# Attention scores with stacked keys and both query halves on every row, and weighted values in one slice

## The chip, the cores and the metric

The kernel runs on one core of a Trainium2 chip. The metric is the device time of one execution in microseconds. Five engines share the work: PE multiplies matrices (PEld is its weight load, a queue of its own in the profile), DVE and ACT do elementwise work, POOL does some elementwise work and issues transfers, SP only issues transfers.

## The reference

Two layers of a diffusion backbone over 256 context tokens and 1024 latent tokens, width 1024. Layer 0 is a pair of recurrent mixers and a mixture of experts; layer 1 is windowed attention and a second mixture of experts. Only the attention of layer 1 is touched:

```
for each block of 128 latent queries, 16 query heads in 4 key groups, head size 64:
    s_loc = q . k          over the latent keys within +-128 tokens (up to 384 keys)
    s_ctx = q . k_ctx      over all 256 context keys
    p     = softmax([s_loc, s_ctx, sink of the head])
    o     = p[:, :window] . v  +  p[:, window:-1] . v_ctx
out = o @ w_out
```

All inputs are f32. The kernel makes most f32 products out of short-significand parts: x is split into hi (x rounded) and lo = x - hi, and hi.hi, hi.lo and lo.hi are added in PSUM.

## The kernel before

Layer 1 is projected token tile by token tile; rotated queries and keys go out to DRAM with channels on rows, two key groups (64 channels each) on the 128 rows of a tile. `keys` brings the keys back in two parts: `k2` holds the hi part of a key group twice, on both row halves, and `kl` the lo part, two groups on one tile. `load_q` brings the queries of a query tile and a pair of key groups: for each group, the hi part stands on the group's own row half and the lo part on the other half.

`Attn.run` goes through 64 steps of one query tile, one key group and two heads each (8 steps for a query tile), and 12 more that finish what is in flight. PE's order is that of the code (a manual schedule); on ACT, DVE and POOL the framework's scheduler sets the order. In a step PE does, in turn:

- the scores of a first head (L1902 against the window's keys, L1903 against the context's), in two passes: `k2` on all 128 rows (hi.hi + lo.hi at once), and then `kl` on the group's 64 rows (hi.lo);
- transposes of probabilities of two steps before (L1937, into `ps_pT`);
- the scores of the second head, and the rest of the transposes;
- a slice of the weighted values (`mix`, L1954, into `ps_av`; the stationary operand has 64 columns). A `mix` serves two steps and comes in two slices, two key blocks in the first and the rest in the second, so every step has one;
- a slice of the output projection of an earlier query tile (`out_tile`, L1345, six products), and now and then transposes, router product (L1396) and affinities of a tile.

Around it, DVE masks and reduces the scores (L1910), ACT takes the exponentials (L1915), DVE and ACT make the scale (L1918 to L1922: a sum on ACT's side, a reciprocal on DVE's), ACT scales one head (L1924) and POOL or DVE the other (L1923). ACT copies the transposes' first and last tile out of PSUM (L1941), DVE the middle one (L1939); they take turns in two PSUM buffers. Once in four steps the next queries are split (ACT L1876, DVE L1877). Behind the fifth query tile DVE also begins the list of best tokens of each expert (L1421 to L1430), a slice in each step.

When the last query tile is through its router (L1396, L1400), DVE makes the second list, rows are gathered, and the second mixture of experts starts; its weights have been loaded ahead.

Of the kernel before, what the change touches and what calls it, by code (L numbers as in the profile page):

```python
# [10 lines left out]
F32R = mybir.dt.float32r  # L11
# [8 lines left out]
D = 1024  # L20
# [11 lines left out]
def step_of(m):  # L32
    """Step at which direction 1 meets chunk m, and the chunk of a step."""
    return 3 - m if m < 4 else 23 - m
# [6 lines left out]
def rows_ap(t, off, rows, cols):  # L41
    """rows x cols view of a contiguous DRAM tensor, from element `off`."""
    return bass.AP(tensor=t.tensor, offset=t.offset + off, ap=[[cols, rows], [1, cols]])
# [12 lines left out]
def log_exp_table(K):  # L56
    """Loads the activation table that serves Ln and Exp together."""
    K.table = K.tc.keep_in_program_order(K.nc.scalar.preload_act_table_set("natural_log_exp_and_others")).ins


def behind(K, ins, name):
    """Keeps an instruction behind the named one in program order."""
    K.tc.add_manual_dep(ins.ins, name, mybir.DependencyInfo(
        mybir.DependencyClass.NoSync, mybir.DependencyReason.DATA), reason="order")


def after_table(K, ins):
    """Keeps an activation behind the last explicit table load."""
    if ins.ins.name not in K.pinned:
        K.pinned.add(ins.ins.name)  # L70
        behind(K, ins, K.table.name)


class Fill:
    """Generators advanced beside a main stream, one slice at a time; lead: instructions they are moved forward."""
# [26 lines left out]
# ---------------------------------------------------------------- constants  # L102
# [4 lines left out]
def consts(K, A):  # L107
# [9 lines left out]
    # per 64-row half: free index minus row index of the half  # L117
# [48 lines left out]
    # silu(c), silu(c_ctx) as [128 d, k, 32] stationaries with two live columns  # L166
# [6 lines left out]
# ---------------------------------------------------------------- ada modulation  # L173
def ada_part(K, A, layer, jj, wp, pp, wtag="adaw", ptag="adap", bufs=2):
    """N-chunks 4jj..4jj+3 of layer's modulation rows: rows 32g (lat), 32g+1 (ctx) of modr[:, jj]."""
# [37 lines left out]
def modcol(K, layer, m, kt, s):  # L213
    """[128,1] column of modulation m for channels 128kt.., stream s (0 lat, 1 ctx)."""
# [4 lines left out]
def mod_bcast(K, layer, m, s, dst):  # L219
    """dst [128, D] <- modulation m of stream s on every partition."""  # L220
# [6 lines left out]
def norm_cols(K, pool, layer, norm, ms, mh, tag):  # L227
    """[128, 2, kt, stream]: gain * (1 + scale), shift of a modulated norm; ms, mh: scale and shift modulations."""
# [11 lines left out]
# ---------------------------------------------------------------- layer-0 input: norm, modulate, transpose  # L240
def head(K, A, hp, hh, hl):
    """hh + hl = modulated RMS norm of [ctx; x], channel layout [128, 8, T]."""
# [61 lines left out]
# ---------------------------------------------------------------- layer-0 projection, column tile by column tile  # L304
def both(nc, out, ps, func, **kw):
    """Activation of a projected column tile (context, latent) into token order."""
# [4 lines left out]
class InProj:  # L311
    """Projected column tiles (first column, continuation), weights loaded two tiles ahead across runs."""
# [28 lines left out]
    def run(self, posts, fills, drain):  # L341
        """Continues the next tiles with posts; fills: (generators, slices per k tile); drain: those to finish."""
# [23 lines left out]
def post_z(K, j, wk, tag, bufs):  # L366
    """Stores the silu of gate tile j."""
# [9 lines left out]
# ---------------------------------------------------------------- RWKV-7 operands  # L377
def store_L(K, unit, n0, x, rev=False):
    """x [(half, s), chunk, t] -> K.s_L [unit, chunk, half, s, t]; chunks n0.. (descending if rev)."""
# [3 lines left out]
class Rwkv:  # L383
    """Token shift, loras, decays and the chunk operands alpha, rho, beta, kappa of both directions.

    With c the running sum of the log decay inside a chunk, in the direction's order:
    alpha = kk e^(c-), rho = r e^c, beta = b e^-c, kappa = k e^-c.
    """
# [26 lines left out]
    def shift(self, ps, j, out):  # L415
        """out = (1 - mu) p + mu/2 (previous + next), zero beyond the ends of each stream."""
# [29 lines left out]
    def invert(self, ct):  # L446
        """Queues the inverses of a column tile once its chunk matrices are traced."""
# [5 lines left out]
    def prep_gen(self, ct):  # L453
# [14 lines left out]
        for bi, (a, m) in enumerate(BLK):  # L468
# [75 lines left out]
            # bonus and gate  # L544
# [28 lines left out]
# ---------------------------------------------------------------- gated DeltaNet operands  # L573
class Gdn:
    """Short convolution, gates and the chunk matrices of the gated delta rule, keys and queries not normalised.

    With nk = 1/|k|: L[t,s] = (k_t.k_s) e^(g_t-g_s) nk_s^2 beta_s, A[t,s] = (q_t.k_s) e^(g_t-g_s) nk_s^2 beta_s,
    r = v/nk - e^g S k, Y = (I+L)^-1 r, o = q S e^g + A Y, S' = e^(gl) S + (k nk^2 beta e^(gl-g))^T Y.
    Rows 0-63 carry direction 0, rows 64-127 direction 1 in flipped token order.
    """  # L580
# [12 lines left out]
    def to_chunks(self, ps, src, w):  # L593
        """ps [(d, p), step, w] <- src [128 token, tile, d, w], direction 1 flipped."""
# [20 lines left out]
    def gates(self, ab):  # L615
# [11 lines left out]
        # softplus(x) = max(x, 0) + ln(1 + e^-|x|)  # L627
# [33 lines left out]
    def conv(self, ps, j):  # L661
        """Five-tap centred convolution over tokens of column tile j."""
# [40 lines left out]
    def sums(self, sq, s, h):  # L703
        """K.ssq[tok, tile, s, h] = sum over channels of the squares, plus eps."""
# [23 lines left out]
    def tok(self, x, h, c0, scaled):  # L728
        """Channel tile x -> token rows of K.s_kv [T, 1024], columns of head h (values divided by nk)."""
# [60 lines left out]
# ---------------------------------------------------------------- inverses of the 32-blocks of I + L  # L790
def inv_blocks(K, c0):
    """The tensor of the inverses of chunk c0, its number of chunks and the place of c0 in it."""
# [3 lines left out]
def tri_inv(K, pool, parts, store, bufs=2):  # L796
    """Inverts the two 32-row diagonal blocks of 64x64 chunk matrices, one block per lane.

    parts: (unit, swap, first chunk, chunks), lanes (chunk, half, q) each. K.s_L holds L^T (L where swap is set);
    K.s_T [form, unit, chunk, half, q, 32, 32] receives the inverse (form 0) and its transpose (form 1), chunks  # L800
    of the context and of the latent tokens apart.
    """
# [38 lines left out]
# ---------------------------------------------------------------- the two scans, chunk by chunk  # L841
def scan_rows(K):
    """K.rows: token rows of each step, rows 0-63 forward, rows 64-127 backward; and rows of K.s_o[0 or 1]."""
# [15 lines left out]
class Scan:  # L859
# [14 lines left out]
    def tri_tile(self, n):  # L874
        """Tile of the inverses of step n, its zero blocks set."""
# [9 lines left out]
    # -- loads  # L885
    def load2(self, m):
        """Channel operands of steps 2m, 2m+1."""
# [24 lines left out]
    def load_tri(self, n):  # L912
        """Inverse blocks of step n."""
# [14 lines left out]
    def load_tok(self, n):  # L928
        """Token operands of step n."""
# [14 lines left out]
    # -- matrices that do not wait for the state  # L944
    def gram(self, n):
        """Chunk products of the RWKV operands of step n, and their operands on token rows; six slices."""
# [32 lines left out]
    def corner(self, n):  # L979
        """The off-diagonal 32-block -T22 L21 T11 of every inverse of step n; six slices."""  # L980
# [161 lines left out]
    def run(self, later, tri):  # L1142
        """All steps; later: called with a load of a later step; tri: inverses that only latent steps need."""
# [31 lines left out]
# slices of a step: r and n the two recurrences, g and c the matrices of the next step between them  # L1175
# [5 lines left out]
# ---------------------------------------------------------------- scan outputs -> mixer output, channel layout  # L1181
def split_hl(K, hi, lo, src):
    """hi = src rounded to the short significand, lo = src - hi."""
# [4 lines left out]
def post_rwkv(K, p, ps, mh, ml, ct, a, m, o):  # L1188
    """Generator: loads, mean, variance and the rest."""
# [26 lines left out]
def post_gdn(K, p, ps, mh, ml, tt, o_):  # L1216
    """Generator: the normed rows, then their turn into channel layout."""
# [27 lines left out]
def turns(posts):  # L1245
    """Slices of the generators of a block (one slice in already), a later one between the two of each."""
# [4 lines left out]
def load_split(K, wp, W, rows, cols, name, parts, bufs=3, tag="wstage", gain=None, stage=None, now=True):  # L1251
    """Resident hi/lo [128, rows/128, cols] of a DRAM matrix; parts: (k tile, partition, nrows, row0) pieces.

    gain: factors of the columns, on every partition; with now False the third result is a generator that loads and
    splits, one k tile a slice.
    """
# [26 lines left out]
def tile_rows(t, tt):  # L1283
    """Rows of token tile tt of a (context, latent) pair of DRAM tensors."""
# [3 lines left out]
def load_raw(K, t, W, last):  # L1288
    """t [128, 8, 1024] <- a square matrix, to be split later; issued behind instruction last."""
# [12 lines left out]
def bcast_mods(K, A, layer, s, cpool, tpool, ps, ms, norm, tag, tb=2, shared=None):  # L1302
    """Modulations ms of stream s on every partition; the first one as norm gain * (1 + scale) if norm is given."""
# [20 lines left out]
def out_tile(K, p, op, ps2, ps1, m, wh, wl, tt, x_src, g2, nrm, router, aff, bufs=2, tb=2, t0=0, halves=False):  # L1324
    """Out projection of token tile tt, residual, FFN norm, router affinities of the tile; a generator.

    Slices: eight of the product, then two turns, the router product and the affinities.

    m(k): hi and lo of channel tile k of the branch; halves: the product is made one half of the columns after the
    other, in one bank.  # L1330
    g2: gate of the branch on every partition, or None where the weights carry it. K.s_h holds the normed rows
    before the modulation nrm.
    """
# [384 lines left out]
class Attn:  # L1718
# [226 lines left out]
    def mix(self, n, pair, jj, pTs):  # L1945
# [5 lines left out]
        for c, ch in enumerate(chunks):  # L1951
# [4 lines left out]
            if c in (1, len(chunks) - 1):  # L1956
                yield
# [381 lines left out]
```

## Time and profile before

| | |
|---|---|
| median of 3 runs | 3622.27 us (3619.68 to 3623.23) |
| span of the profiled execution | 3620.5 us |
| what lies around it, median less span | 1.8 us |
| mean granted TensorE clock | 0.943 |
| busy: PE, DVE, ACT, POOL | 92%, 67%, 57%, 20% |
| attention steps, first scores to the end of the last ones | 2563 to 2942 us |

The time of the profiled execution is not listed apart from its span; 1.8 us is taken for what lies around it. PE's busy share counts pipelined matmuls with modelled ends, so what a matmul costs PE is read from the distance between starts, not from its duration. PEclk 1.00 is 2.4 GHz, 0.50 is 1.2 GHz.

### The profile page before, as it was taken

What the parts mean: (1) busy time and instruction counts of PE and PEld (TensorE: products, weight loads), DVE (VectorE), ACT (ScalarE), POOL (GpSimd) and SP (SyncE); (2) the same over time, 40 slices, a digit from 0 to 9 for tenths busy, and PEclk for the clock granted to TensorE, in tenths of its full rate; (3) what the DMA queues carried; (4) which work ended last, traced back from release to release, by engine and by line L of the source; (5) the groups of instructions that cost most, each with busy time, mean ns of one, the idle gap of its engine ahead of it and who ended that gap; (6) DMA issues with size and microseconds to landing.
All of it is one profiled execution on the core that took longest, in us unless ns stands there. A gap on an engine that the chain in (4) does not pass through costs nothing. (4 is left out here: it accounts for less than half of the span.)

```text
span 3620.5 us, 60293 instructions
## 1 busy us (share of the span) xinstructions
PE 3343.5 (92%) x23392; PEld 2475.0 (68%) x23392; DVE 2421.4 (67%) x4034; ACT 2073.4 (57%) x3529; POOL 731.6 (20%) x716
## 2 busy tenths in 40 slices
PE   5999999996999979699999999899899986999997
PEld 3866667775888867566666666567667764888885
DVE  4267774667343356967777777644666588999998
ACT  4244554332333356376666666453577745888886
POOL 1233322222322244111111100101223310101001
PEclk8999999996999989899999999999699997999998
DMA  5255565666897756468888887663311138999995
GB/s 190 70 190 172 183 204 172 225 187 126 172 210 162 162 167 209 152 245 282 282 288 278 284 286 265 202 230 123 77 39 44 47 110 306 378 396 386 394 375 217
DMA packets 480161, 767.80 MB, mean 212 GB/s; under 512 B 231836, under 2 KB 318532, under 8 KB 472708
## 3 DMA queue, kind: packets, MB, share of 16 engines
q1 hardware_dynamic: 434640, 601.05, 50.2%
q0 software_dynamic: 41648, 151.55, 13.5%
q10 hardware_dynamic: 3587, 11.36, 1.0%
q8 instruction: 184, 3.01, 0.3%
q14 instruction: 102, 0.83, 0.1%
HBM read 631.48 MB, written 132.38 MB: 211 GB/s over the span
## 5 line engine op out<-in xcount | busy, mean ns | idle before, releaser
L1185 DVE TENSOR_TENSOR ulo<-raw,uhi 128x1024 fp32r<-128x1024 f32 x768 | 901.6, 1222 | 127.6 <-ACT uhi L1184 118.9
L1184 ACT ACTIVATE uhi<-raw 128x1024 fp32r<-128x1024 f32 x768 | 789.4, 1069 | 245.2 <-PE ps_y L1624 127.0
L1573 PE MATMUL ps_h<-uhi,xh 128*128 128x512 f32 x1024 | 333.7, 404 | 1.4 <-ACT uhi L1184 1.3
L1573 PE MATMUL ps_h<-ulo,xh 128*128 128x512 f32 x1024 | 320.4, 393 | 3.0 <-DVE ulo L1185 1.0
L1573 PE MATMUL ps_h<-uhi,xl 128*128 128x512 f32 x1024 | 319.0, 392 | 0.0
L1640 POOL DMA_INDIRECT s_x<-yo,idxl x31 | 49.2, 1587 | 977.1 <-DVE yo L1636 977.1
L1573 PEld LDWEIGHTS ps_h<-uhi,xh 128*128 128x128 f32 x1024 | 184.0, 188 | 73.5 <-ACT uhi L1184 21.4
L1573 PEld LDWEIGHTS ps_h<-ulo,xh 128*128 128x128 f32 x1024 | 190.6, 188 | 54.9 <-DVE ulo L1185 12.4
L1573 PEld LDWEIGHTS ps_h<-uhi,xl 128*128 128x128 f32 x1024 | 191.2, 188 | 41.5
L354 PE MATMUL ps_in<-hl,whi 128*128 128x512 f32 x512 | 172.2, 411 | 0.0
L354 PE MATMUL ps_in<-hh,wlo 128*128 128x512 f32 x512 | 169.4, 409 | 1.5 <-POOL wlo L338 1.5
L354 PE MATMUL ps_in<-hh,whi 128*128 128x512 f32 x512 | 169.5, 408 | 0.9 <-DVE convu L671 0.9
L1624 PE MATMUL ps_y<-uhi,th 128*128 128x512 f32 x512 | 167.2, 407 | 0.6 <-ACT tc L1610 0.5
L1624 PE MATMUL ps_y<-ulo,th 128*128 128x512 f32 x512 | 161.1, 395 | 0.1
L1624 PE MATMUL ps_y<-uhi,tl 128*128 128x512 f32 x512 | 158.7, 391 | 0.0
L1910 DVE CUSTOM_DVE_ANT_0 pe<-ps_s,amask,sink 128x640 f32<-128x640 f32 (+2 forms) x128 | 104.4, 816 | 66.7 <-PE ps_s L1903 65.0
L966 DVE TENSOR_TENSOR ar<-ps_g,strict 64x256 f32<-64x256 f32 x80 | 33.8, 422 | 154.2 <-PE ps_g L964 153.9
L1923 POOL TENSOR_SCALAR pe<-pe,ast 128x640 f32<-128x640 f32 (+1 forms) x48 | 92.1, 1919 | 215.1 <-DVE ast L1922 193.7
L1546 ACT ACTIVATE xv<-ps_x,Gf 128x128 f32<-128x128 f32 x256 | 96.7, 471 | 66.7 <-PE ps_x L1542 66.7
L1579 PE MATMUL ps_hc<-raw,xc 128*32 128x512 f32 x1024 | 126.1, 599 | 0.0
L1624 PEld LDWEIGHTS ps_y<-uhi,th 128*128 128x128 f32 x512 | 91.1, 188 | 49.7 <-issue 20.1
L1345 PE MATMUL ps_out<-woh,mh 128*128 128x512 f32 x288 | 117.6, 454 | 0.0
(509 smaller groups left out, 7548.9 us busy)
## 6 DMA issues: line engine op xcount, KB each, us to landing
raw<-in_moe_w_dram SPq DMA_DIRECT2D x384, 1024.0 KB
ada_w<-in_ada_w_dram SPq DMA_DIRECT2D x48, 1024.0 KB
wraw<-in_e_w_in_dram SPq DMA_DIRECT2D x32, 512.0 KB
s_rk<-arbk POOLq DMA_DIRECT2D x16, 1024.0 KB, 5.7
kq<-s_kq SPq DMA_DIRECT2D x20, 512.0 KB
s_x<-ox POOLq DMA_DIRECT2D x18, 512.0 KB
s_h<-ot POOLq DMA_DIRECT2D x18, 512.0 KB, 4.1
s_rkv<-rkv POOLq DMA_DIRECT2D x12, 640.0 KB, 3.9
```

The costliest lines, as they stand in the source:

```text
L354: nc.tensor.matmul(ps, l[:, k, :], r[:, k, a:a + m], start=(k == 0 and n == 0), stop=(k == 7 and n == 2))
L966: nc.vector.tensor_mul(ar[orow, hp, :, cd[d]], pg[orow, :, 0:64], K.strict[orow, d:d + 1, :].to_broadcast([64, 4, 64]))
L1184: K.nc.scalar.activation(hi, src, AF.Copy)
L1185: K.nc.vector.tensor_sub(lo, src, hi)
L1345: nc.tensor.matmul(po[:, cp_], l, r[:, k, c_], start=(k == 0 and n == 0), stop=(k == 7 and n == 2))
L1546: nc.scalar.activation(v[:, q], pt[:, q], AF.Identity, bias=self.nrm[:, 1, k, 0:1], scale=self.nrm[:, 0, k, 0:1])
L1573: nc.tensor.matmul(pl[m][n], l[:, k], r[:, 512 * n:512 * n + 512], start=(k == 0 and i == 0), stop=(k == 7 and i == 2))
L1579: nc.tensor.matmul(pc[32 * g:32 * g + 32], xc[:, k_], rs[g // 2][:, 512 * (g % 2):512 * (g % 2) + 512], start=(k_ == 0), stop=(k_ == 7), s ...
L1624: nc.tensor.matmul(py[n], l[:, k], r[:, 512 * n:512 * n + 512], start=(k == 0 and i == 0), stop=(k == 7 and i == 2))
L1640: nc.gpsimd.indirect_dma_start(out=K.s_x[1], out_offset=bass.IndirectOffsetOnAxis(ap=idx[:, e:e + 1], axis=0), in_=yo, in_offset=None, com ...
L1910: nc.vector.tensor_tensor_reduce(pe[:, a:b], sc[:, 512 - nl + a:512 - nl + b], self.mask[:, m:m + b - a], 1.0, low, OP.add, OP.min, st[:, ...
L1923: (nc.vector if n < NV else nc.gpsimd).tensor_scalar(pes[0][:, :nk], pes[0][:, :nk], st[:, 4, 0:1], None, op0=OP.mult)
```

## The change

The keys of a group stand as hi on the group's own row half and lo on the other half, in one tile; `kl` is gone. The queries of a group stand as hi on both halves and, in a second tile, as lo on both halves. The scores are two passes over all 128 rows: queries hi against keys (hi.hi + hi.lo), then queries lo against the same keys (lo.hi, and lo.lo, which was left out before). Each load of queries has two ACT copies and two DVE subtractions for a group instead of one each; each part of the keys has one ACT copy less for a group. `mix` makes all its products in one slice, so of two steps one has them all and the other none, and what follows a `mix` comes one step earlier.

```diff
@@ keys
-            self.kl = p.tile([128, 2, T], F32R, name="kl", bufs=1)
...
-                r = slice(64 * par, 64 * par + 64)
-                for half in range(2):
-                    nc.scalar.activation(self.k2[64 * half:64 * half + 64, 2 * a + par, c], t[r], AF.Copy)
-                nc.vector.tensor_sub(self.kl[r, a, c], t[r], self.k2[r, 2 * a + par, c])
+                r, o = slice(64 * par, 64 * par + 64), slice(64 * (1 - par), 64 * (1 - par) + 64)
+                nc.scalar.activation(self.k2[r, 2 * a + par, c], t[r], AF.Copy)
+                nc.vector.tensor_sub(self.k2[o, 2 * a + par, c], t[r], self.k2[r, 2 * a + par, c])
@@ load_q
-        q2 = p.tile([128, 2, 4, 128], F32R, name="q2", tag="q2", bufs=2)
+        q2 = p.tile([128, 2, 2, 4, 128], F32R, name="q2", tag="q2", bufs=2)
...
-            nc.scalar.activation(q2[r, g], t[r], AF.Copy)
-            nc.vector.tensor_sub(q2[o, g], t[r], q2[r, g])
+            for x in (r, o):
+                nc.scalar.activation(q2[x, 0, g], t[r], AF.Copy)
+            for x in (r, o):
+                nc.vector.tensor_sub(q2[x, 1, g], t[r], q2[r, 0, g])
@@ probs
-            qa = q2[:, gg, 2 * jj + i_]
-            for i, (l, r) in enumerate(((qa, self.k2[:, g]), (qa[hr], self.kl[hr, pair]))):
-                nc.tensor.matmul(sc[:, 512 - nl:512], l, r[:, k0:k0 + nl], start=(i == 0), stop=(i == 1))
-                nc.tensor.matmul(sc[:, 512:768], l, r[:, 0:NCTX], start=(i == 0), stop=(i == 1))
+            k2 = self.k2[:, g]
+            for i in range(2):
+                qa = q2[:, i, gg, 2 * jj + i_]
+                nc.tensor.matmul(sc[:, 512 - nl:512], qa, k2[:, k0:k0 + nl], start=(i == 0), stop=(i == 1))
+                nc.tensor.matmul(sc[:, 512:768], qa, k2[:, 0:NCTX], start=(i == 0), stop=(i == 1))
@@ mix
-            if c in (1, len(chunks) - 1):
-                yield
+        yield
@@ run, mix_step
-            mx, left, key, jj_ = mixes[0]
-            if left == 2 and jj_ == 0:
+            mx, key, jj_ = mixes.pop(0)
+            if jj_ == 0:
                 self.av = pso.tile([128, 4, 128], F32, name="ps_av", tag="av")
-            next(mx, None)
-            mixes[0][1] -= 1
-            if left == 1:
-                mixes.pop(0)
-                if jj_ == 1:
+            next(mx)
+            if jj_ == 1:
...
```

PE in the middle of the attention, the scores of a first head between an output-projection slice and the transposes. Before:

```order
L1345 MATMUL ps_out<-woh,ml 128x512
L1902 MATMUL ps_s<-k_22547,q_24430 128x384
L1903 MATMUL ps_s<-k_22547,q_24430 128x256
L1902 MATMUL ps_s<-kl,q_24430 128x384
L1903 MATMUL ps_s<-kl,q_24430 128x256
L1937 MATMUL ps_pT<-ident,pe 128x128 x4
```

Now (the lines have moved by one; `k_22547` now holds hi and lo):

```order
L1345 MATMUL ps_out<-woh,ml 128x512
L1903 MATMUL ps_s<-k_22547,q_24477 128x384
L1904 MATMUL ps_s<-k_22547,q_24477 128x256
L1903 MATMUL ps_s<-k_22547,q_24477 128x384
L1904 MATMUL ps_s<-k_22547,q_24477 128x256
L1938 MATMUL ps_pT<-ident,pe 128x128 x4
```

The number of products and their columns are as before; the second pass no longer takes another tile on half of the rows. Behind the second head's scores the two steps of a `mix` read on PE, before:

```order
L1937 MATMUL ps_pT<-ident,pe 128x128 x6
L1954 MATMUL ps_av<-pT,v 64x256 x4
L1345 MATMUL ps_out<-woh,mh 128x512
...
L1937 MATMUL ps_pT<-ident,pe 128x128 x6
L1954 MATMUL ps_av<-pT,v 64x256 x6
L1345 MATMUL ps_out<-woh,mh 128x512
```

and now:

```order
L1938 MATMUL ps_pT<-ident,pe 128x128 x6
L1955 MATMUL ps_av<-pT,v 64x256 x10
L1345 MATMUL ps_out<-woh,mh 128x512
...
L1938 MATMUL ps_pT<-ident,pe 128x128 x6
L1345 MATMUL ps_out<-woh,mh 128x512
```

The ten products stand in one step, and in the other the projection follows the transposes at once. (A product shown here is two records in the profile.) On ACT, the queries of a load in the middle of the attention, before:

```order
L1924 ACTIVATE pe<-pe,ast 128x640
L1320 ACTIVATE rst<-rst 128x1
L1876 ACTIVATE q_24430<-qld 64x512 x2
L1941 ACTIVATE pT<-ps_pT 128x512
L1915 ACTIVATE pe,ast<-pe,ast 128x640
```

and now, a step and a half of it:

```order
L1942 ACTIVATE pT<-ps_pT 128x512
L1916 ACTIVATE pe,ast<-pe,ast 128x640
L1875 ACTIVATE q_24477<-qld 64x512
L1942 ACTIVATE pT<-ps_pT 128x256
L1916 ACTIVATE pe,ast<-pe,ast 128x640
L1920 ACTIVATE ast<-ast 128x2
L1875 ACTIVATE q_24477<-qld 64x512
L1391 ACTIVATE ohT<-ps_hT,Gf_22896 128x128 x4
L1925 ACTIVATE pe<-pe,ast 128x640
```

Of the four copies of a load, one now stands between the two exponentials of a step and ahead of a copy of transposes, others stand between the sum (L1920, before L1919) and the scaling (L1925, before L1924).

## Rows read from the trace of the kernel before

**Rows 1.** Busy time by engine in three stretches of the attention: stretch, length, busy (instructions).

```profile
core 0: us, PE busy (x) PEld busy (x) DVE busy (x) ACT busy (x) POOL busy (x), PEclk, DMA share, GB/s
2563.20:2633.60 70.40, 65.30 (x250) 43.05 (x251) 57.77 (x117) 44.55 (x95) 21.33 (x10) 0.59 0.29 76
2633.60:2900.50 266.90, 266.90 (x1623) 187.50 (x1622) 163.84 (x432) 196.44 (x461) 83.71 (x50) 1.00 0.12 41
2900.50:2942.30 41.80, 41.78 (x260) 30.33 (x258) 35.87 (x123) 26.24 (x69) 12.10 (x10) 1.00 0.11 39
```

**Rows 2.** The same stretches, line L1902 alone: four products are one step.

```profile
2563.20:2633.60 70.40, 27.55 (x48) 13.59 (x49) 0.59 0.29 76
2633.60:2900.50 266.90, 72.78 (x176) 32.77 (x177) 1.00 0.12 41
2900.50:2942.30 41.80, 11.44 (x32) 5.76 (x31) 1.00 0.11 39
```

**Rows 3.** PE and PEld in order of time, one step: start, duration, instruction, [idle before].

```profile
2748.02 0.19 PEld L1902 LDWEIGHTS ps_s<-k,q 128*128 128x128 f32 x1
2748.02 0.39 PE L1345 MATMUL ps_out<-woh,ml 128*128 128x512 f32 x1
2748.24 0.34 PE L1902 MATMUL ps_s<-k,q 128*128 128x384 f32 x1
2748.41 0.28 PE L1903 MATMUL ps_s<-k,q 128*128 128x256 f32 x1
2748.62 0.18 PEld L1902 LDWEIGHTS ps_s<-kl,q 64*128 64x128 f32 x1 [0.19 <-issue]
2748.62 0.44 PE L1902 MATMUL ps_s<-kl,q 64*128 64x384 f32 x1
2748.90 0.27 PE L1903 MATMUL ps_s<-kl,q 64*128 64x256 f32 x1
2749.10 0.66 PE L1937 MATMUL ps_pT<-ident,pe 128*128 128x128 f32 x4
2749.51 0.42 PE L1902 MATMUL ps_s<-k,q 128*128 128x384 f32 x1
2749.77 0.28 PE L1903 MATMUL ps_s<-k,q 128*128 128x256 f32 x1
...
2750.46 0.88 PE L1937 MATMUL ps_pT<-ident,pe 128*128 128x128 f32 x6
```

**Rows 4.** PE in order of time around the two slices of a `mix`.

```profile
2756.45 0.87 PE L1937 MATMUL ps_pT<-ident,pe 128*128 128x128 f32 x6
2757.26 1.08 PE L1954 MATMUL ps_av<-pT,v 128*64 128x256 f32 x8
2758.27 0.50 PE L1345 MATMUL ps_out<-woh,mh 128*128 128x512 f32 x1
2758.61 0.39 PE L1345 MATMUL ps_out<-wol,mh 128*128 128x512 f32 x1
...
2762.80 1.52 PE L1954 MATMUL ps_av<-pT,v 128*64 128x256 f32 x12
```

**Rows 5.** Groups of 2633.6 to 2900.5 on ACT and DVE: busy, mean ns, idle before.

```profile
L1924 ACT ACTIVATE pe<-pe,ast 128x640 f32<-128x640 f32 x46 | 38.1, 829 | 18.9 <-DVE ast L1922 18.9
L1876 ACT ACTIVATE q<-qld 64x512 fp32r<-64x512 f32 x23 | 14.3, 623 | 0.2
...
L1877 DVE TENSOR_TENSOR q<-qld,q 64x512 fp32r<-64x512 f32 x22 | 15.1, 686 | 0.7
```

**Rows 6.** PE in order of time: the first two heads' scores of the attention.

```profile
2563.24 0.58 PE L1902 MATMUL ps_s<-k,q 128*128 128x256 f32 x1 [1.01 <-ACT qst L1831]
...
2564.69 0.58 PE L1902 MATMUL ps_s<-k,q 128*128 128x256 f32 x1
```

**Rows 7.** The key operands by tile: count, duration ns min/median/max, first and last start.

```profile
L1751 ACT ACTIVATE k<-kT x16: 732/735/739, 2492.1 to 2559.5; 64x640 fp32r<-64x640 f32 x16
```

**Rows 8.** DVE in order of time: first token list's start and end, last tile's router.

```profile
2899.64 0.82 DVE L1421 MAX8 tk<-aff 16x8 f32<-16x640 f32 x1
...
2976.34 0.21 DVE L1430 TENSOR_SCALAR tk<-tk 16x128 f32<-16x128 f32 x1
...
2982.82 0.17 DVE L1400 TENSOR_REDUCE sm<-ps_rt 128x1 f32<-128x16 f32 x1 [6.27 <-PE ps_rt L1396]
```

**Rows 9.** Busy time in the stretch of that token list, columns as in rows 1.

```profile
2899.60:2976.50 76.90, 70.94 (x422) 51.40 (x420) 69.64 (x202) 38.70 (x98) 17.23 (x14) 1.00 0.29 101
```

**Rows 10.** The same for one expert of the second mixture of experts.

```profile
3168.50:3203.60 35.10, 34.99 (x160) 28.49 (x160) 32.60 (x33) 29.73 (x39) 3.10 (x2) 1.00 1.03 393
```

More of the change, by code (lines that the diff above doesn't have):

```diff
@@ L1892, in probs @@
         st = p.tile([128, 5, 2], F32, name="ast", tag="ast", bufs=4)
-        hr = slice(64 * gg, 64 * gg + 64)
         h0 = 4 * g + 2 * jj
@@ L1980, in mix_step @@
                 return
-            mx, left, key, jj_ = mixes[0]
-            if left == 2 and jj_ == 0:
+            mx, key, jj_ = mixes.pop(0)
+            if jj_ == 0:
                 self.av = pso.tile([128, 4, 128], F32, name="ps_av", tag="av")
-            next(mx, None)
-            mixes[0][1] -= 1
-            if left == 1:
-                mixes.pop(0)
-                if jj_ == 1:
-                    mh, ml = (p.tile([128, 4, 128], F32R, name=x, tag=x, bufs=3) for x in ("mh", "ml"))
-                    split_hl(self.K, mh, ml, self.av)
-                    m[key] = mh, ml
-                    if key[1] == 1:
-                        outs.append([out(key[0], [m.pop((key[0], x)) for x in range(2)]), 0])
+            next(mx)
+            if jj_ == 1:
+                mh, ml = (p.tile([128, 4, 128], F32R, name=x, tag=x, bufs=3) for x in ("mh", "ml"))
+                split_hl(self.K, mh, ml, self.av)
+                m[key] = mh, ml
+                if key[1] == 1:
+                    outs.append([out(key[0], [m.pop((key[0], x)) for x in range(2)]), 0])
         ng = self.load_q(0, 0)
@@ L2030, in run @@
                 else:
-                    mixes.append([self.mix(ty, pair_, jj_, (first, pT)), 2, (ty, pair_), jj_])
+                    mixes.append([self.mix(ty, pair_, jj_, (first, pT)), (ty, pair_), jj_])
             if i % 4 < 3:
```

## The prediction

> **What bounds the kernel now.** I read the stretches first: the change touches the attention alone, and a busy share of the whole span says nothing about it. The 64 steps fall into three stretches [rows 1, 2]. The first 12 (48 products of L1902, four to a step) take 70.4 us at a granted clock of 0.59, with PE idle for 5.1 us of it and DVE for 12.6. The next 44 take 266.9 us, 6.07 us a step, at the full clock, and PE has no idle time at all, while ACT is idle 70.5 us (1.60 a step) and DVE 103. The last 8 take 41.8 us; PE is full there too, and DVE is busy for 35.9.
>
> So PE sets the time of the 44 steps. What it does in one I read from the order of time, by distances between starts, since the durations overlap [rows 3]. The first head's scores go from 2748.24 to the transposes at 2749.10: 0.86 us. The first two products, on all rows, are 0.17 apart, and the second one, of 256 columns, should then need little more than 0.12 (twelve records of 256 columns and eight differ by four records and 1.52 - 1.08 = 0.44 us, so 0.11 each [rows 4]). It takes 0.21 until the next product starts. The weight load of that next product, the one on 64 rows, was idle for 0.19 us with nothing to wait for, and starts together with its product, whereas the load for the first product starts with the projection's last product, 0.22 us ahead of its own. So when the pass goes from 128 rows to 64, the load does not run beside the product before it; and again on the way back (0.28 and 0.20 for the two products on 64 rows). The second head, behind transposes, takes 0.95 (2749.51 to 2750.46), as its first interval is 0.26.
>
> A `mix` slice shows the same at its ends [rows 4]. Six transposes take 0.81 us before it, where four before a score take 0.41, which is 0.62 for six: 0.19 more. The slice of eight records takes 1.01, eight times 0.11 is 0.88: 0.13 more. The first product of the projection behind it takes 0.34 against 0.22 [rows 3]: 0.12 more. That is 0.44 for a slice.
>
> **The change, part by part.** *Scores on PE.* Without the changes of rows a head costs 0.17 + 0.12 + 0.17 + 0.12 = 0.58 us, and 0.67 behind transposes. Against 0.86 and 0.95 that is 0.28 a head, 0.56 a step. If the first weight load of the transposes then also hides behind the last product (one transpose is 0.41 / 4 = 0.10), it is 0.38 a head, 0.76 a step. *The mix.* One slice of 0.44 in two steps goes, 0.22 a step; where the projection now follows transposes directly, its first product may take the 0.09 by which 0.26 is above 0.17: 0.17 a step. Together PE has 0.73 to 0.98 us less in a step of 6.07.
>
> One rule of the Trainium skill speaks against that. "TensorE: Matmul & The Clock Gate", in the section "The mechanism" under "Packing small matmuls", says that a weight load overlaps a running product only when their row groups differ. By it the change would lose 0.13 us a head (worked out with the rivals) where the rows give a gain of 0.28. The trace disagrees: the load of 2748.02 and its predecessor's product are both on 128 rows and start together [rows 3].
>
> *The queries.* Each load, once in four steps, has two more ACT copies of 0.623 us and two more DVE subtractions of 0.686 [rows 5]: 0.31 and 0.34 us a step. They are hidden by ACT's 1.60 and DVE's 2.3 idle us of a step as long as PE is the longest. But the step shrinks too, so ACT becomes the next bound: 1.60 - 0.31 = 1.29 us of idle time are left, and of that 0.43 a step (18.9 / 44) is ACT waiting for DVE's reciprocal, a round trip that a shorter PE does not remove. So ACT allows 0.86 to 1.29, by how much of the trip the copies now placed there fill. PE allows 0.73 to 0.98. With two engines that close, one step with all of a `mix` and one with none, and only two buffers for the transposes, some of it is lost: in the short step PE runs ahead, and its last transposes stand behind ACT's copy of the first ones, which waits in ACT's queue behind an exponential or a scaling (0.83 us [rows 5]). A copy that comes 0.6 us late in one of two steps costs 0.3 a step. I take **0.70 a step**, near PE's lower bound less a little, with 0.40 and 0.98 as ends: 44 x 0.70 = **31 us** (18 to 43).
>
> *The first 12 steps.* At half clock a head takes 1.45 us [rows 6], four products of 256 columns at twice 0.11 are 0.88, so PE could give 0.57 x 24 = 14 us. But DVE has 12.6 us idle here, and three loads of queries add 3 x 1.37 = 4.1, so it allows at most 8.5, and PE already waits for others in 5.1 us. I take half, **4 us** (0 to 9).
>
> *The last 8 steps and the 12 that finish.* PE's gain is the same 0.73 to 0.98 a step, but DVE is busy with the first token list from 2899.64 to 2976.34 [rows 8], 69.6 of 76.9 us [rows 9], and the last tile's router finds it idle only for 6.27 us. The list starts when a tile's affinities are there and moves forward with them. So up to 7.3 + 6.3 us can be taken out between the two before DVE is the bound, less 1.4 for a load: 12 us, and PE would take out 8 x 0.85 = 7. Placement will cost some: I take **4 us** (0 to 8). In the finishing steps five slices of a `mix` become fewer by two at 0.44: **1 us**.
>
> *The keys.* The second part of the keys stands between the projection and the first scores. Four ACT copies of 0.735 [rows 7] go there, 2.9 us; the first scores wait for ACT [rows 6], but for its query copy, with DVE's rotation between. I take **2 us** (0 to 3). The first part lies beside the projection and costs nothing: PE works on there.
>
> Behind the attention all that follows waits for the last tile's router, and an expert keeps PE busy for 34.99 of 35.10 us [rows 10], from weights loaded ahead, so it moves forward whole and gives nothing back.
>
> Sum: 31 + 4 + 4 + 1 + 2 = 42 us, off the profiled span of 3620.5 and the 1.8 us around it, which is the median of 3622.3: **3580 us**. The ends add up to 18 + 0 + 0 + 0 + 0 = 18 and 43 + 9 + 8 + 1 + 3 = 64: 3604 and 3558.
>
> **The rivals.** *ACT takes over the bound* (a wait in place of the one removed). For it: 196.4 + 44 x 0.31 = 210 us of ACT work against 266.9 - 31 = 236, 89%, in one fixed order with a copy of queries ahead of a copy of transposes. Against it: its idle time now is mostly waiting for PE. If a step gains 0.15 to 0.40 only, that is 7 to 18 us there and about 4 elsewhere: 3600 to 3612, say 3605.
>
> *DVE gives it back at the end*: if the token list ends later than the last router, the 7 us of the last 8 steps and part of the 31 stay in DVE's queue. That needs the list to be late by more than its 6.27 us of slack; it would cost 5 to 10 us and end at about 3588, inside the main case's range.
>
> *The clock* (the other side). In the first 12 steps the granted clock was 0.59 with PE busy for 65.3 of 70.4 us, so busy does not mean full clock. If PE, now waiting for ACT, were granted 1.2 GHz in the later steps, a step would take twice the distances above: two heads at 2 x 0.58, ten transposes at 0.20, ten records of a `mix` at 0.22, six projection products at 0.44, or 2.3 + 2.0 + 2.2 + 2.6 = 9.1 us, 3.0 above today's and 3.7 above the forecast. Twelve such steps use up the gain of 42; twenty would give 3580 + 74 = 3654. Against it: in an expert DVE and ACT work nearly as long as PE and in turn with it, and the clock is 1.00 [rows 10].
>
> *Loads that do not hide*: if a load on 128 rows could not run beside a product on 128 rows, four loads of 0.10 would stand open in each head, 0.58 + 0.41 = 0.99 us against 0.86, so 128 heads lose 0.13 each and the slices still gain 0.2 x 52: 3622 + 17 - 10 = 3629. The load of 2748.02 speaks against it [rows 3]. This is the rule of "TensorE: Matmul & The Clock Gate" above.
>
> *The change does little*: if the 0.2 us gaps come from the alternation of the two products' banks and not of rows, only the `mix` gains: 3622 - 10 = 3612.
>
> **How the numbers follow.** Main case (with the late list) 0.66, ACT as the bound 0.20, gaps that stay 0.05, the clock 0.04, loads 0.02, more than 64 us 0.03. Leaving out the last four and the upper part of the ACT case, the range is 3557 to 3606. A change below 0.2% (7 us) cannot be told from none with this kernel: slower 0.05, within 0.03, faster 0.92.
>
> **What would show it.** Right: starts of the scores' products 0.17, 0.12, 0.17, 0.12 apart, no idle time of the load ahead of the second pass, steps of about 5.4 us, PE with a few short waits for ACT's copies of transposes, the full clock from the thirteenth step on, and the same 35.1 us an expert. Wrong: distances of 0.2 that stay; long PE waits for ACT; a granted clock under 1.00 between the thirteenth step and the end of the attention; a router wait on DVE behind the first list.

## The result and the profile after

The changed kernel takes 3594.7 us (median of 4 runs, 3592.2 to 3602.1) against 3622.7 (3619.7 to 3623.2): ratio 0.993, 95% interval 0.9914 to 0.9946. The profiled execution took 3594.87 us, its span is 3593.0 (27.5 less than before), the mean granted clock 0.947. The forecast was 3580 us in 3557 to 3606: faster, as said, but the gain is 28 us instead of 42.

Where the 27.5 us of span came from is read from the same stretches as before, from the first scores to step 12, to step 56, and to the last scores. Busy time by engine in them, columns as in [rows 1], after:

```profile
2563.10:2625.70 62.60, 45.58 (x256) 36.26 (x257) 58.16 (x119) 45.40 (x99) 20.41 (x10) 0.78 0.34 89
2625.70:2877.90 252.20, 235.08 (x1623) 192.02 (x1623) 177.10 (x458) 205.64 (x481) 81.62 (x49) 1.00 0.12 44
2877.90:2917.20 39.30, 37.33 (x270) 30.06 (x269) 36.67 (x127) 29.76 (x75) 13.11 (x10) 1.00 0.12 41
```

and of line L1903 alone (L1902 before), 48, about 176 and 32 products as in [rows 2], so the stretches hold the same work:

```profile
2563.10:2625.70 62.60, 18.69 (x48) 11.67 (x49) 0.78 0.34 89
2625.70:2877.90 252.20, 60.01 (x177) 33.19 (x177) 1.00 0.12 44
2877.90:2917.20 39.30, 9.13 (x32) 5.86 (x31) 1.00 0.12 41
```

Against [rows 1]:

| stretch | before | after | gained | forecast |
|---|---|---|---|---|
| up to the first scores | 2563.2 | 2563.1 | 0.1 | 2 |
| first 12 steps | 70.4 | 62.6 | 7.8 | 4 |
| next 44 | 266.9 | 252.2 | 14.7 | 31 |
| last 8 | 41.8 | 39.3 | 2.5 | 4 |
| from there to the end | 678.2 | 675.8 | 2.4 | 1 |

The products do what was forecast. PE in order of time with the first three loads of PEld, one step of after, which answers to [rows 3]:

```profile
2688.63 0.39 PE L1345 MATMUL ps_out<-woh,ml 128*128 128x512 f32 x1
2688.63 0.19 PEld L1903 LDWEIGHTS ps_s<-k,q 128*128 128x128 f32 x1
2688.85 0.34 PE L1903 MATMUL ps_s<-k,q 128*128 128x384 f32 x1
2688.85 0.19 PEld L1904 LDWEIGHTS ps_s<-k,q 128*128 128x128 f32 x1
2689.02 0.28 PE L1904 MATMUL ps_s<-k,q 128*128 128x256 f32 x1
2689.03 0.19 PEld L1903 LDWEIGHTS ps_s<-k,q 128*128 128x128 f32 x1
2689.14 0.34 PE L1903 MATMUL ps_s<-k,q 128*128 128x384 f32 x1
2689.31 0.28 PE L1904 MATMUL ps_s<-k,q 128*128 128x256 f32 x1
2689.43 0.60 PE L1938 MATMUL ps_pT<-ident,pe 128*128 128x128 f32 x4
2689.79 0.42 PE L1903 MATMUL ps_s<-k,q 128*128 128x384 f32 x1
...
2690.46 0.38 PE L1938 MATMUL ps_pT<-ident,pe 128*128 128x128 f32 x2
```

The starts are 0.17, 0.12, 0.17 and 0.12 apart, so a head takes 0.58 us, and the second 0.67, to the hundredth what was forecast; each load shown starts with the product before it. But in the 44 steps PE, which had no idle time before, is now idle for 252.2 - 235.08 = 17.1 us. What it waits for there (engine, line, what it waited for: us in total, times, longest):

```profile
PE ps_pT L1938 <- ACT pT L1942: 13.3, 20, 1.2
PE ps_pT L1938 <- ACT ohT L1391: 3.4, 5, 0.7
PE ps_pT L1938 <- DVE pe L1924: 0.4, 1, 0.4
```

All 20 waits for that copy stand in steps with a whole `mix`, the long ones. Two of them, lines chosen from all engines in order of time:

```profile
2682.67 0.60 PE L1938 MATMUL ps_pT<-ident,pe 128*128 128x128 f32 x4
...
2683.06 0.16 DVE L1923 RECIPROCAL ast<-ast 128x2 f32<-128x2 f32 x1
...
2683.32 0.83 ACT L1925 ACTIVATE pe<-pe,ast 128x640 f32<-128x640 f32 x1 [1.00 <-DVE ast L1923]
...
2683.70 0.60 PE L1938 MATMUL ps_pT<-ident,pe 128*128 128x128 f32 x4
...
2684.05 0.57 ACT L1942 ACTIVATE pT<-ps_pT 128x512 f32<-128x512 f32 x1
...
2684.68 0.44 PE L1938 MATMUL ps_pT<-ident,pe 128*128 128x128 f32 x2 [0.39 <-ACT pT L1942]
...
2704.02 1.06 ACT L1318 ACTIVATE ot<-ox 128x1024 f32<-128x1024 f32 x1 [0.82 <-DVE ox L1349]
...
2704.60 0.60 PE L1938 MATMUL ps_pT<-ident,pe 128*128 128x128 f32 x4
...
2705.08 0.81 ACT L1925 ACTIVATE pe<-pe,ast 128x640 f32<-128x640 f32 x1
...
2705.80 0.57 ACT L1942 ACTIVATE pT<-ps_pT 128x512 f32<-128x512 f32 x1
...
2706.42 0.44 PE L1938 MATMUL ps_pT<-ident,pe 128*128 128x128 f32 x2 [1.22 <-ACT pT L1942]
```

The transposes of a step come in three tiles (begun at 2682.67, 2683.70 and 2684.68 in the first place), and there are two buffers. So the third tile must wait until ACT has copied the first one out (2684.05). PE made the first from 2682.67 on; but ACT takes up the scaling of the step before ahead of the copy, and that had waited for DVE's reciprocal of 2683.06, 1.00 us long, and ran from 2683.32. The `mix` of 2.4 us, which needs no such buffer, stands behind the third tile, so nothing covers the wait. In the second place a tile's norm (L1318), itself waiting for DVE, pushes scaling and copy back further: 1.22 us. That ACT's queue is strictly first in, first out is what the Trainium skill says ("PSUM — Partial Sum Buffer", section "Engine vs sequencer instructions"); the trace agrees, the copy coming behind scaling and norm in both places, though no row here catches ACT idle with a copy ready.

The other rows that the prediction rested on: the first scores, the end of the token list and the last router on DVE, and one expert, each from its own view:

```profile
2563.16 0.58 PE L1903 MATMUL ps_s<-k,q 128*128 128x256 f32 x1 [0.74 <-ACT qst L1829]
```

```profile
2949.81 0.22 DVE L1430 TENSOR_SCALAR tk<-tk 16x128 f32<-16x128 f32 x1
2955.12 0.17 DVE L1400 TENSOR_REDUCE sm<-ps_rt 128x1 f32<-128x16 f32 x1 [5.09 <-PE ps_rt L1396]
```

```profile
3141.40:3176.50 35.10, 34.94 (x161) 28.44 (x161) 32.59 (x33) 29.73 (x39) 3.09 (x2) 1.00 1.03 387
```

The first scores still wait for ACT's query copy, the list ends ahead of the last router with 5.09 us of idle time left (6.27 before [rows 8]), and an expert takes the same 35.1 us as before [rows 10].

### The profile page after: what moved, and what is told of

Its sections match the earlier page's. It is cut to its first block, busy times and chain, and to the rows that moved or that the text cites. A ratio compares the mean times of both kernels' runs of the same rounds, so it can differ in the third digit from the quotient of the medians.

```text
span 3593.0 us, 60363 instructions
## 1 busy us (share of the span) xinstructions
PE 3285.6 (91%) x23392; PEld 2471.3 (69%) x23392; DVE 2437.1 (68%) x4066; ACT 2082.9 (58%) x3553; POOL 730.4 (20%) x716
## 5 line engine op out<-in xcount | busy, mean ns | idle before, releaser
L1924 POOL TENSOR_SCALAR pe<-pe,ast 128x640 f32<-128x640 f32 (+1 forms) x48 | 90.4, 1883 | 184.8 <-DVE ast L1923 94.0
L1938 PE MATMUL ps_pT<-ident,pe 128*128 128x128 f32 x608 | 96.8, 284 | 31.5 <-ACT pT L1942 14.6
```

The lines of the kernel that those rows point to most:

```text
L1924: (nc.vector if n < NV else nc.gpsimd).tensor_scalar(pes[0][:, :nk], pes[0][:, :nk], st[:, 4, 0:1], None, op0=OP.mult)
L1938: nc.tensor.transpose(pt[:, k, i_], pes[i_][:, 128 * (c + k):128 * (c + k) + 128], K.ident)
```

## The experiments

Theory A: PE gained what was forecast, and lost about 17 to 20 us of it again to one wait, the one for ACT's copy in the uneven long step. Rival B: ACT, with 205.6 us of work in 252.2, is the new bound, and any other order of the same work ends at about the same time. Rival C: the added query copies are what costs. The kernel before took 3604.1 us beside the first four runs and 3622.7 to 3622.9 beside the others, so only ratios are compared between these sets. A ratio is known to about 0.2%, 7 us; smaller differences are read from the 44 steps. "44 steps" is the middle stretch of [rows 1], from the same step to the same step; with the change it took 252.2 and, once more, 251.9 us. A step is measured from its first product of scores to that of the next.

**The scores alone.** Keys, queries and scores changed, `mix` in two slices as before; against the changed kernel, without the lines of `mix_step` that go with it:

```diff
             nc.tensor.matmul(po[...], ...)
-        yield
+            if c in (1, len(chunks) - 1):
+                yield
```

> The scores as changed, the weighted values in two slices as before, so that every step has one slice. If the loss is PE waiting, in the step that has the whole mix, for ACT's copy of the first transposes (two PSUM buffers in turn), even steps remove most of that wait: steps 12 to 55 gain 0.55 to 0.75 us each (24 to 33 us) and 3580 to 3588 in all, faster than the changed kernel. If ACT's own work (with the added copies of queries) is the bound, the waits stay and the time is 3594 to 3604, the mix's 10 us lost on top.

3574.8 us, ratio 0.9917 (0.9893 to 0.9941), 44 steps 247.0. Its middle stretch, columns as in [rows 1], and PE's waits there:

```profile
2605.90:2852.90 247.00, 241.90 (x1622) 190.84 (x1621) 174.41 (x454) 206.71 (x482) 84.94 (x50) 1.00 0.13 45
```

```profile
PE ps_pT L1938 <- ACT pT L1942: 4.9, 11, 0.6
```

In these steps that is five us less than with the whole change, although PE has more to do: with a slice in each step the wait shrinks from 13.3 us to 4.9. It does not vanish, and the steps gain 19.9 us where 24 to 33 were expected. As a whole this kernel cannot be told from the changed one (0.992 and 0.993), so neither time expected was met. In the 44 steps the scores carry the gain, and the one slice, as the change orders it, gives part of it back.

**The mix alone.** The kernel before with `mix` and `mix_step` changed; the part in `mix`:

```diff
-            if c in (1, len(chunks) - 1):
-                yield
+        yield
```

> The scores as before, the weighted values in one slice. By the distances of the prediction a slice less in two steps is worth 0.17 to 0.22 us a step: 3612. If uneven steps make PE wait for ACT's copy even without the added copies of queries, most of that is lost: 3617 to 3623.

3595.1 us, ratio 0.9971 (0.9956 to 0.9986), 44 steps 265.4. PE waits for the same copy here where it waited for nothing before:

```profile
PE ps_pT L1937 <- ACT pT L1941: 4.5, 10, 0.4
```

So uneven steps bring the wait even without the added query copies. They are not its only source: the scores alone had 4.9 us of it with a slice in every step, and the two halves together have 13.3, more than their sum. By its ratio this run is at the first value expected (3612 against 3622), by its 44 steps, which gain 1.5 us, at the second. From the first scores to the end its trace is 2.7 us shorter than that of before (3593.9 - 2539.3 against 3620.5 - 2563.2), so most of the 9 us between the medians does not show in the part that was changed.

**The last transposes in a third place.** Every score tile has an unused quarter; the third tile of transposes goes into that of the second head:

```diff
-            sc = ps.tile([128, 1024], F32, name="ps_s", tag="sc")
+            sc = self.sc = ps.tile([128, 1024], F32, name="ps_s", tag="sc")
...
-            pt = ps1.tile([128, 2, 2, 128], F32, name="ps_pT", tag="aux")
+            if c == 4:
+                pt = self.sc[:, 768:1024].rearrange("p (k i t) -> p k i t", k=1, i=2)
+            else:
+                pt = ps1.tile([128, 2, 2, 128], F32, name="ps_pT", tag="aux")
```

> The changed kernel, but the last transposes of a head pair go to the unused quarter of the score tile's second bank, so that they wait for no copy of the first ones. If that wait is what PE loses (16.7 us of idle time in steps 12 to 55, about 22 by distances), 12 to 22 us go: 3573 to 3583. If ACT is the bound by itself, PE waits at another place instead, and the time stays at 3590 to 3596.

3603.0 us, ratio 0.9993 (0.9978 to 1.0008), 44 steps 273.5. PE's largest wait in them:

```profile
PE ps_s L1941 <- DVE ast L1911: 31.1, 44, 1.2
```

The wait for ACT's copy is gone, but a new one took its place: the transposes now wait in every step until DVE has reduced the second head's scores in that tile. Neither time expected came, and this run says nothing between A and B.

**The copies swapped.** DVE copies the first tile of transposes, ACT the second:

```diff
-            if c == 2:
+            if c == 0:
                 nc.vector.tensor_copy(pT[:, c:c + w], pt[:, :w])
```

> The changed kernel, but DVE copies the first transposes out of PSUM and ACT the second ones. If the wait is for ACT's queue, DVE (69% busy in steps 12 to 55) comes to the first copy sooner and PE's wait at the last transposes falls: 3578 to 3588. If DVE's queue, with two reductions a step ahead, is no sooner, the wait has DVE's name: 3592 to 3600.

3571.3 us, ratio 0.9904 (0.9883 to 0.9926), but 44 steps 251.2, as with the change. PE now waits for DVE in place of ACT:

```profile
PE ps_pT L1938 <- DVE pT L1940: 7.8, 22, 0.9
```

The wait changes its engine, and the 44 steps stay as long: the steps with a whole `mix` take 7.17 us instead of 7.70, the others 4.24 instead of 3.76. The ratio falls in the first range expected and the wait's name is that of the second; the ratio's interval meets that of the change, and from the first scores to the end the trace takes 1028.6 us against 1029.9. The swap moves the wait and is not shown to remove any of it.

**The change once more**, as a reference:

> The changed kernel itself, beside the kernel before on this chip, to have it beside the experiments: ratio 0.993 as measured first, 0.991 to 0.995.

3592.1 us, ratio 0.992 (0.9906 to 0.9934), 44 steps 251.9, and PE waits 13.1 us for ACT's copy in 20 times: all repeats.

**The mix ahead of the third transposes.** One call of PE's order moved, all work the same:

```diff
             if new:
                 next(pg[i])
+            mix_step()
             if tg:
                 pT = next(tg)
...
-            mix_step()
```

> The changed kernel with one edit of PE's order: the weighted values of a step stand ahead of its last transposes instead of behind them, so that PE works for 2.3 us while ACT copies the first ones. No engine has more or less to do. If PE's loss is that wait, most of the 20 us that steps 12 to 55 lose by it go: 0.987 to 0.989 of the kernel before. If ACT as a whole is the bound, PE waits elsewhere and the ratio stays at 0.992 to 0.994.

3574.1 us, ratio 0.987 (0.985 to 0.9891). The middle stretch and PE's largest wait there:

```profile
2623.20:2856.50 233.30, 231.87 (x1623) 191.90 (x1622) 171.62 (x458) 205.49 (x481) 82.17 (x49) 1.00 0.14 47
```

```profile
PE ps_pT L1938 <- ACT pT L1942: 1.0, 5, 0.2
```

A long step of it, PE and ACT in order of time:

```profile
2664.53 0.60 PE L1938 MATMUL ps_pT<-ident,pe 128*128 128x128 f32 x4
...
2665.56 0.84 ACT L1925 ACTIVATE pe<-pe,ast 128x640 f32<-128x640 f32 x1
...
2666.28 0.60 ACT L1942 ACTIVATE pT<-ps_pT 128x512 f32<-128x512 f32 x1
2666.31 2.38 PE L1955 MATMUL ps_av<-pT,v 128*64 128x256 f32 x20
...
2668.62 0.44 PE L1938 MATMUL ps_pT<-ident,pe 128*128 128x128 f32 x2
```

ACT's copy still starts 1.75 us after the first of its transposes, behind a scaling, but PE spends the time on the `mix`. The 44 steps fall from 252.2 to 233.3, 18.9 us, with the same 205.5 us of work on ACT. The steps with a whole `mix` take 6.73 us instead of 7.70, the others 3.88 instead of 3.76. A holds, B falls.

**The last transposes in the first head's tile**, whose reduction DVE has done earlier; the diff is that of the second head's tile, but for `self.sc`, which is set for the first head only:

> As the third buffer, but in the score tile of the step's first head, which DVE has read by then, where the second head's made PE wait for DVE's reduction (28 us). If the wait for ACT's copy is the loss and this place is free, 12 to 20 us go: 0.987 to 0.990. If the transposes still wait for DVE's reduction of the first head, or the next step's scores for ACT's copy, nothing is won: 0.993 to 1.000.

3574.8 us, ratio 0.9874 (0.9857 to 0.989), 44 steps 235.6. Of PE's waits there, only 2.4 us for `ohT` are left. A second way to take the same wait away gives nearly the same time.

**The query copies alone.** The kernel before, with each ACT copy and each DVE subtraction of a query group made twice:

```diff
-            nc.scalar.activation(q2[r, g], t[r], AF.Copy)
-            nc.vector.tensor_sub(q2[o, g], t[r], q2[r, g])
+            for _ in range(2):
+                nc.scalar.activation(q2[r, g], t[r], AF.Copy)
+            for _ in range(2):
+                nc.vector.tensor_sub(q2[o, g], t[r], q2[r, g])
```

> The kernel before, with the copy and the subtraction of each query group made twice: the added work of the change without its gain. PE is the bound there and ACT idle 1.6 us a step, so this should cost nothing: 0.998 to 1.002. If the added copies stand in the way by their place in ACT's and DVE's queues alone, 44 steps lose 0.1 to 0.3 us: 1.001 to 1.004.

3625.1 us, ratio 1.0007 (0.9995 to 1.0019), 44 steps 268.0 against 266.9. ACT does 207.1 us of work in them instead of 196.4, and PE has no wait. C falls for a PE that sets the pace; and the moved `mix` above has the added copies too, with PE busy for 231.87 of 233.3 us.

**Two slices, ahead of the third transposes.** The first experiment with the moved `mix_step()`:

> The changed scores with the mix in two slices as before, and the slice put ahead of the third transposes. The question is what one slice instead of two is worth once PE no longer waits for the copy. If the price of a slice's two ends (0.2 to 0.25 us a step, 0.44 in two steps, as read from the kernel before) is real, the 44 middle steps take 9 to 11 us more than the 233 of the version with one slice ahead of the third transposes, 242 to 244, and the ratio is about 0.990. If it is not, and one slice is worth nothing, the 44 steps take 233 to 236 here too, ratio about 0.987. If the two slices, being even, let PE run with no wait at all while one slice still leaves some, it may be as low as 230.

3584.8 us, ratio 0.9891 (0.9874 to 0.9908), 44 steps 239.1. With the wait for the copy gone here (2.3 us for `ohT` are left) and all but gone there (1.0), one slice is worth 239.1 - 233.3 = 5.8 us, 0.26 for each of 22 slices less; 0.8 of the 5.8 is a difference in PE's idle time. The two kernels are not of the same set, but the last one below, of the same set as this one, takes 232.7. That is neither of the two expected values: less than 9 to 11, more than nothing. Against before, the scores alone bring 266.9 - 239.1 = 27.8 us here, 0.63 a step.

**Moved mix and swapped copies together:**

> The mix ahead of the third transposes, and in addition DVE copies the first transposes and ACT the second. Theory that the wait for the copy of the first transposes was all that PE lost: it is gone already, so the 44 steps stay at 233 (230 to 236) and the ratio at 0.987. Rival, ACT as the next bound beside PE: the copy by ACT of the first transposes still holds something up in the short step, and taking it to DVE brings a further 3 to 8 us (ratio 0.985).

3582.8 us, ratio 0.9888 (0.9868 to 0.9908), 44 steps 241.2, worse than the moved mix alone by 7.9 us. PE is idle for 6.0 of them (1.4 with the moved mix alone), and what it waits for most is DVE's copy:

```profile
PE ps_pT L1938 <- DVE pT L1940: 3.1, 5, 0.9
```

Neither theory expected a loss. It stands in the steps without a `mix`, which take 4.25 us instead of 3.88; the others stay at 6.71 (6.73 before the swap). One such step, with the moved mix alone:

```profile
2641.09 0.60 ACT L1942 ACTIVATE pT<-ps_pT 128x512 f32<-128x512 f32 x1 [1.18 <-PE ps_pT L1938]
...
2641.48 0.82 PE L1938 MATMUL ps_pT<-ident,pe 128*128 128x128 f32 x6
```

and with the copies swapped as well:

```profile
2648.63 0.69 DVE L1940 COPY pT<-ps_pT 128x512 f32<-128x512 f32 x1
2648.65 1.16 PE L1938 MATMUL ps_pT<-ident,pe 128*128 128x128 f32 x6
...
2649.37 0.20 PEld L1938 LDWEIGHTS ps_pT<-ident,pe 128*128 128x128 f32 x2 [0.37 <-DVE pT L1940]
```

In the short step no `mix` covers the copy. ACT's starts 0.39 us ahead of the second tile of transposes, and the six transposes of the last two tiles take 0.82 us. DVE's starts with them, the load of the third tile waits for it, and they take 1.16. That is 0.34 in a short step, 7.5 us in 22, and the list of waits shows it in part only.

**Moved mix and the first head's tile together:**

> The mix ahead of the third transposes, and in addition the last transposes go into the unused quarter of the first head's score tile, so that no step has a ring of two for three. Theory that nothing is left of the wait: 44 steps at 231 to 235, ratio 0.985 to 0.988, no better than either alone. Rival, that the two remove different waits and add up: 44 steps below 229, ratio 0.983 or less.

3576.3 us, ratio 0.987 (0.9851 to 0.9889), 44 steps 232.7. The two remove the same wait: together they bring no more than either alone, and nothing of it is left. The moved `mix` is the simplest version that beats both kernels: 0.987 against 0.992 to 0.993.

## Why the prediction was right in kind and off in size

**The 44 steps: the step that failed.** "A copy that comes 0.6 us late in one of two steps costs 0.3 a step. I take 0.70 a step, near PE's lower bound less a little." The price of the products was right: 0.73 to 0.98 us less for PE in a step, and with the wait removed the steps gain (266.9 - 233.3) / 44 = 0.76. The mechanism of the loss was named too, but put into the short step, where PE runs ahead; all 20 waits stand in the long one, from which the moved `mix` took 0.98 us. And it was hardly subtracted: 0.70 leaves 0.03 to 0.28 for it, and it cost 18.9 / 44 = 0.43. By the traces two things go with that size: between the first and the third tile PE now has 0.67 us of scores instead of 0.95 [rows 3], so the change itself took away cover; and ACT's copy is late by a chain (reciprocal on DVE, scaling, copy), not by one instruction. The halves of the change had 4.5 and 4.9 us of the wait each, both together 13.3; no run varied the cover or the chain by itself. The forecast 31 us became 14.7, below even the low end of 18. That the total still lies in its range is owed to the other parts, which gave 12.8 us where the low ends counted on none: a miss upward in the first 12 steps made up for some of this one.

**One `mix` slice.** Priced at 0.44 us, or 0.17 to 0.22 a step; the removed slices measured 0.26 each, 0.13 a step. The rest of the PE gain is the scores': 0.63 against 0.56 to 0.76.

**The first 12 steps.** I halved DVE's limit of 8.5 us because PE already waited for others; the gain was 7.8. DVE's idle time fell from 12.6 to 62.6 - 58.16 = 4.4 us, and its waits for scores from 9.8 to 2.3, so the steps went to nearly that limit. The 4.1 us put in for three loads were 2.8 for two, and DVE's busy time rose by 0.4 only. PE, busy for 45.6 us instead of 65.3, is now the one that waits. The granted clock was 0.78 instead of 0.59, which was not forecast; how much of the 7.8 is owed to it no run separates.

**The keys.** Forecast 2 us, measured 0.1 from the start of the span. But where the projection ends varies from run to run: its last product starts at 2556.28 before and at 2556.98 after. From there to the first scores it is 6.96 us before and 6.18 after, 0.8 less; 6.88 and 6.62 in the two other runs with the old keys, 5.67 to 6.28 in all ten with the new ones. So the keys gained about 0.7 us, still far from 2. What stands ahead of the first scores is DVE's rotation, among DVE's four subtractions of the keys. DVE in order of time, before:

```profile
2559.52 0.81 DVE L1752 TENSOR_TENSOR kl<-kT,k 64x640 fp32r<-64x640 f32 x1
2560.25 0.75 DVE L1815 TENSOR_TENSOR rot<-rot 128x256 f32<-128x256 f32 x2
2561.03 0.82 DVE L1752 TENSOR_TENSOR kl<-kT,k 64x640 fp32r<-64x640 f32 x1
```

and after:

```profile
2559.60 0.82 DVE L1750 TENSOR_TENSOR k<-kT,k 64x640 fp32r<-64x640 f32 x1
2560.43 0.76 DVE L1813 TENSOR_TENSOR rot<-rot 128x256 f32<-128x256 f32 x2
```

Before, three of the subtractions stand ahead of the rotation and the fourth behind it; after, all four stand ahead of it, which takes back 0.8 us. "With DVE's rotation between" was written in the prediction and not followed through; this is read from the traces, no run tested it.

**The last 8 and the finishing steps.** 2.5 and 2.4 against 4 and 1, together the forecast 5. PE, full there before, is idle for 2.0 us of the last 8.

**The rivals.** ACT as the bound: its price (3600 to 3612) was the nearer one for the 44 steps (14.7 lies in its 7 to 18), but its mechanism falls, since ACT does the same work in 233.3 us. It was one late copy, not a full engine. The late list: idle time of 5.09 us ahead of the last router, so it did not happen. The clock: 1.00 from step 12 on. Gaps that stay: the distances are 0.17 and 0.12 in the step shown.

Loads that do not hide: the load of 2688.85 starts with the product of 2688.85, both on all 128 rows. By "TensorE: Matmul & The Clock Gate" of the Trainium skill, section "The mechanism", a load overlaps only a product on other row groups; the trace disagrees with that sentence, with four products in 0.58 us. The same section also lets a load go ahead into the background weight buffer, and no run here shows whether that is what happens. "TensorEngine Tiling (Array Packing)" of the Trainium skill, section "Key Properties", says that a change of the tiling mode drains the engine; the trace agrees as far as it goes: without the change of rows a head takes 0.28 us less. That it was a drain that took them is not shown.

## What to carry to other kernels

When a change makes the work of the limiting engine uneven between steps, look at the shortest ring of buffers in the long step, and put work that needs no buffer of that ring between the producer that fills it and the one that needs the first place again. If the forecast names a wait and its price, subtract it in full. A wait is not proof that the engine waited for is full: whether reordering alone removes it tells the two apart, at the price of one moved call.

## What the runs showed of the hardware

In the first 12 steps a shorter busy time of PE went with a higher granted clock: busy for 65.3 of 70.4 us at 0.59 before, for 45.6 of 62.6 at 0.78 after; 0.71 to 0.80 in the ten traces with the changed scores, 0.59 to 0.67 in the three without. The products are as many, and at the lower level they take longer (in the trace of after, 256 columns take 0.21 us from start to start at 2563.76 and 0.12 at 2689.02), so this does not say which comes first. Before, a stretch of 34.2 us in these steps ran at 0.50 (1.2 GHz) with PE busy for 33.74 of them:

```profile
2593.80:2628.00 34.20, 33.74 (x119) 20.82 (x120) 29.86 (x53) 22.21 (x46) 12.08 (x5) 0.50 0.27 69
```

What sets the clock there was not tested.

The same kernel before took 3604.1 us in one set of runs and 3622.7 in the others, a shift of 0.5%, and the first scores in the traces of the first set start some 20 us earlier (2537.4 to 2541.1 against 2556.3 to 2568.6), ahead of nearly all that was changed. An absolute time from one set cannot be held against another; the stretches can, and the ratios within their intervals.
